# One decoder step: two triples of the gated convolution ahead of q, k, v, and five live delta units

## The chip, the cores and the metric

The kernel runs on one core of one Trainium2 chip. The metric is the device time of one execution in microseconds; lower is better. The core has five engines that take their instructions each from a queue of its own: TensorE (matmuls, PE in the profile, its weight loads PEld), VectorE (DVE), ScalarE (ACT), GpSimd (POOL) and SyncE (SP, which only starts transfers). TensorE writes to PSUM, eight banks that DVE and ACT read; all else lies in SBUF.

## The reference

One layer is computed for 256 prompt tokens and 8 decoding sequences of 4 tokens (288 columns), all in fp32, model width 2048:

```
x += 0.5 * post(SwiGLU_1(pre(x)))
h  = pre(x); P = h @ w_in        # columns [B | C | hc | q | k | v | z | a | b]
y_A = B * dwconv3(C * hc)        # gated convolution, 1024 channels
y_B = gated delta rule over silu(dwconv4(q, k, v)), 8 heads of 128, then rmsnorm * silu(z)
x += post(concat(y_A, y_B) @ w_out)
x += 0.5 * post(SwiGLU_2(pre(x)))
x += post(sigmoid(pre(x) @ w_ple_gate) * (p @ w_ple_proj))
```

B, C, hc, q, k, v and z are each eight blocks of 128 columns. The delta rule goes over chunks of tokens and needs, for each chunk and head, the inverse of a triangular matrix:

```
S_t = e^{g_t} S_{t-1} (I - b_t k_t k_t^T) + b_t k_t v_t^T,   o_t = S_t^T q_t
```

The new states of both convolutions and of the delta rule are outputs too.

## The kernel before

Activations lie transposed: 128 channels on the partitions, 288 tokens along the row. Every weight matrix is cut into 128 x 128 tiles, and the host lays them out in the order in which they are used, four tiles to a chunk of 256 KB. `Feed` loads chunks on SP's queue, six buffers deep, and splits each: ACT copies it in a rounded form (hi, line 133), DVE subtracts (lo, line 134); four split buffers. A tile costs three matmuls of 288 columns, hi with the high and the low part of the activations (lines 361 and 362) and lo with the high part (line 364), so a chunk costs twelve. `gemm_steps` (line 328) goes through the chunks; a block of columns m has a PSUM accumulator while its 16 row tiles k run, and then `done(m, ...)` reads it. Before the matmuls of a chunk it may advance a generator `extra` by some steps (line 352). `gemm_order` (line 66) puts the first `group` blocks of a matrix k by k, so that work may start while the normalised input is still being made, and the others block by block, four chunks each.

Mixing runs four gemms. `qkv` has 24 blocks in the order k, q, v of head 0, of head 1 and so on, the first six k by k; `qkv_done` (line 597) multiplies by the norm's row, pads (`padded`, line 553), applies four taps (`conv`, line 566: the first on ACT, three on DVE, line 572) and SiLU. A side product `ab` runs with the first block. `conv` has 24 blocks in triples (C, hc, B of one t), block by block; `conv_done` (line 1024) makes C times the squared row (`gc`, line 1028), hc times that with padding, two taps on DVE, times the row (`cr`, lines 1036 and 1037, on POOL), and at last B times `cr` into Y (line 1039). `z` has 8 blocks. Then `out` multiplies by w_out.

Beside them goes the delta rule as the generator `delta` (line 907). It waits until `ab` is done, waits 16 steps, computes the gates, makes the products k k^T and k q^T of the heads that are done (`products`, line 709), and after the last q, k, v block: scales, then `solve` (line 725), which inverts the 32-wide diagonal parts of 16 matrices at once, row after row, all on DVE (lines 736 to 757, the last makes GXT), and next to it `decode`, the two units of the decoding tokens with their states S loaded on POOL's queue (line 849). Only when the solve is through do the 16 prompt units start. A unit (line 826) is a chain of 9 or 10 steps: transposes (line 834), T from GXT on DVE (line 768) with its transpose p0 (line 774), five small products (`invert`, line 764), the new values (line 877), outputs and states (lines 882, 893). Live generators take turns, one step each, and at most LIVE = 4 live at once. During `qkv` a chunk advances the work by one step; during `conv` and `z` every second chunk (EVERY) advances it by RATE x EVERY = 4 steps. What is left after z runs on its own.

PSUM: five banks tagged `acc` for accumulators, three tagged `sm`; every fourth bank of a unit comes from `acc` (`unit_bank`, line 205). The program is written in this order, but a planner sets the final order on each engine by its own costs and by when operands are ready: an engine may take an instruction ahead of earlier ones that are not ready in the planner's reckoning. On the chip each engine then keeps to its queue.

Of the kernel before, what the change touches and what calls it, by code (L numbers as in the profile page):

```python
# [7 lines left out]
F32 = mybir.dt.float32  # L8
F32R = mybir.dt.float32r
AF = mybir.ActivationFunctionType  # L10
ALU = mybir.AluOpType
# [17 lines left out]
RAW_BUFS = 6  # L29
SPLIT_BUFS = 4  # L30
GROUP = 5
WIDE = 7
RATE = 2
LIVE = 4
EVERY = 2
PROJ = ((0, 3), (3, 6), (6, 8))
FILL = 3
QUIET = 32
# [34 lines left out]
def orders():  # L73

    gu = []
    for q in range(NQ):
        gu += gemm_order(range(q * 2 * QF, (q + 1) * 2 * QF), KD, WIDE if q == 0 else 0)
    qkv = [m for h in range(H) for m in (32 + h, 24 + h, 40 + h)]  # L80
    conv = [m for t in range(8) for m in (8 + t, 16 + t, t)]
    return {
        "gu": gu,
        "dn": [(m, q * QF + k) for q in range(NQ) for m in range(KD) for k in range(QF)],
        "qkv": gemm_order(qkv, KD, GROUP + 1),
        "conv": gemm_order(conv, KD, 0),
        "z": gemm_order(range(48, 56), KD, 0),
        "out": gemm_order(range(KD), KD, GROUP),
        "proj": gemm_order(range(KD), 2, 0),
        "gate": gemm_order(range(KD), KD, WIDE),  # L90
    }
# [54 lines left out]
def tile_hymba_step(ctx: ExitStack, tc: tile.TileContext, a: dict):  # L146
# [18 lines left out]
    SA = pers.tile([P, 8, NB, 2], F32, name="SA")  # L165

    plan = []
    for name in ("ffn1", "proj0", "qkv", "conv", "z", "out", "proj1", "ffn2", "proj2", "gate"):
        if name[:4] == "proj":
            plan.append((a["proj"], range(*PROJ[int(name[4])])))  # L170
            continue
        if name[:3] != "ffn":
            plan.append((a[name], range(a[name].shape[0])))
            continue
        for q in range(NQ):
            for w in (a["gu" + name[3]], a["dn" + name[3]]):
                n = w.shape[0] // NQ
                plan.append((w, range(q * n, (q + 1) * n)))
# [26 lines left out]
    def unit_bank(name):  # L205

        turn[0] += 1
        if turn[0] % 4:
            return small(name)
        return psum.tile([P, 512], F32, tag="acc", bufs=ACCS, name=name)  # L210

# [116 lines left out]
    def gemm_steps(order, kt, rhs, done, prep=None, extra=None, rate=0, side=None, every=1, fill=(), fine=False):  # L328

        acc, seen, ready = {}, {}, 0
        for c in range(len(order) // CH):
            if prep:
                if c == 0:
                    prep(0)
                    ready = 1
                    feed.split(0)
                if ready == KD:  # L340
                    prep.after()
                upto = max(k for _, k in order[: (c + LEAD) * CH])
                while ready <= upto:
                    prep(ready)
                    ready += 1
                if c == 0:
                    feed.behind = prep.first
                    for _ in fill:
                        pass
                    feed.behind = None  # L350
            hi, lo = feed.next()
            for _ in range(rate * every if c and c % every == 0 else 0):
                next(extra, None)
            for i in range(CH):
                m, k = order[c * CH + i]
                if m not in acc:
                    acc[m] = small(f"acc{m}") if len(acc) >= ACCS else psum.tile([P, 512], F32, tag="acc", bufs=ACCS, name=f"acc{m}")
                    seen[m] = 0
                xh, xl = rhs(k)
                o = acc[m][:, :N]  # L360
                nc.tensor.matmul(o, hi[:, i, :], xh, start=seen[m] == 0, stop=False)  # L361
                nc.tensor.matmul(o, hi[:, i, :], xl, start=False, stop=False)  # L362
                seen[m] += 1
                nc.tensor.matmul(o, lo[:, i, :], xh, start=False, stop=seen[m] == kt)  # L364
# [256 lines left out]

    def dtile(tag, shape=(P,), bufs=LIVE):
        return dl.tile([P, *shape], F32, tag=tag, bufs=bufs, name=tag)
# [137 lines left out]
    S1, started = {}, set()  # L761
    updates = []

    def invert(u, T, TT):

        col = slice(u, u + 1)
        L = LQ[:, u, 0, :]
# [6 lines left out]
        nc.tensor.transpose(p0[:, 0:P], T, ID)  # L774
        nc.scalar.copy(TT, p0[:, 0:P])
        yield
        B = dtile("B")
        nc.gpsimd.memset(B, 0.0)
        ev = lambda x: x.rearrange("p (a i b) -> p a i b", a=2, i=2)[:, :, 0, :]
        od = lambda x: x.rearrange("p (a i b) -> p a i b", a=2, i=2)[:, :, 1, :]  # L780
# [45 lines left out]
    def unit(u):  # L826
# [3 lines left out]
        vT = VD[:, 4 * w : 4 * w + 4, :].rearrange("p h t -> p (h t)") if dec else V[:, h, n * P : (n + 1) * P]  # L830
        col = slice(u, u + 1)
        T, TT = dtile("T"), dtile("TT")
        pt = unit_bank("pt")
        nc.tensor.transpose(pt[:, 0:P], vT, ID)
        nc.tensor.transpose(pt[:, P : 2 * P], kq[:, 0, :], ID)
# [2 lines left out]
        nc.scalar.activation(rv, pt[:, 0:P], AF.Copy, scale=BRK[:, col])  # L838
        nc.scalar.activation(kd, pt[:, P : 2 * P], AF.Copy, scale=KDC[:, col])
        yield  # L840
        yield from (invert4 if dec else invert)(u, T, TT)

        qs = None
        if dec:
# [25 lines left out]
                nc.tensor.matmul(pS[c], kq[:, c, :], S1[h], start=True, stop=True)  # L870
        if dec or n == 1:
            nc.vector.scalar_tensor_tensor(rv, pS[0], CKS[:, col], rv, op0=ALU.mult, op1=ALU.add)
            qs = dtile("qs", bufs=2)
            nc.scalar.activation(qs, pS[1], AF.Copy, scale=EGC[:, col])
            yield
        pn = unit_bank("pn")
        nc.tensor.matmul(pn[:, 0:P], TT, rv, start=True, stop=True)  # L877
        vn = dtile("vnD", bufs=2) if dec else dtile("vn")
        nc.scalar.copy(vn, pn[:, 0:P])
        yield  # L880
        po = unit_bank("po")
# [131 lines left out]
        yield from proj  # L1013
        keep(0, PJ0)

    gemm(ORD["qkv"], KD, x_parts, qkv_done, mix, work, 1, ab_side, fill=fill_mix())
    mrow = mix.value


    r2 = tmp.tile([P, N], F32, tag="diag", bufs=1, name="r2")  # L1020
    nc.vector.tensor_tensor(r2, mrow, mrow, op=ALU.mult)
    part = {}

    def conv_done(m, ps):
        t = m % 8
        if m // 8 == 1:
            part["g"] = tmp.tile([P, N], F32, tag="e1", name="gc")
            nc.vector.tensor_tensor(part["g"], ps, r2, op=ALU.mult)
        elif m // 8 == 2:
            e, dec = padded(ps, part.pop("g"), SA[:, t, :, :], 2)  # L1030
            nc.gpsimd.tensor_copy(CAP[:, t, :], e[:, SEQ : SEQ + 2])
            nc.gpsimd.tensor_copy(SA[:, t, :, :], dec[:, :, 4:6])
            cp, cd = conv(e, CAW[:, t, :], 2)
            part["c"] = b = tmp.tile([P, N], F32, tag="e0", name="cr")
            seq = lambda x: x[:, SEQ:N].rearrange("p (b t) -> p b t", b=NB)
            nc.gpsimd.tensor_tensor(b[:, 0:SEQ], cp, mrow[:, 0:SEQ], op=ALU.mult)
            nc.gpsimd.tensor_tensor(seq(b), cd, seq(mrow), op=ALU.mult)
        else:
            nc.vector.tensor_tensor(Y[:, t, :], ps, part.pop("c"), op=ALU.mult)

    gate_load = marks[-1]
    gemm(ORD["conv"], KD, x_parts, conv_done, None, work, RATE, every=EVERY)
    nc.gpsimd.dma_start(a["conv_qkv_p"], CQP)
    nc.gpsimd.dma_start(a["conv_qkv_s"], SQ)
    nc.gpsimd.dma_start(a["conv_a_p"], CAP)
# [10 lines left out]
        nc.scalar.activation(VD[:, h, :], t[:, SEQ:N], AF.Silu)  # L1056
        finished.append(m)

    gemm(ORD["z"], KD, x_parts, z_done, None, work, RATE, every=EVERY)
    for _ in work:  # L1060
        pass
    YH = big.tile([P, 2, 8, N], F32R, tag="H", name="YH")
# [189 lines left out]
```

## Time and profile before

| | |
|---|---|
| median of 3 runs | 2382.6 us (2380.88 to 2384.11) |
| profiled execution | 2383.07 us, its span 2381.3 us |
| granted TensorE clock, mean | 0.997 |
| instructions in the span | 47494 |
| HBM read, written | 386.68 MB, 9.26 MB |

The span runs from the first to the last instruction. The page gives for every engine its busy time and its share of the span. A stretch from 40 equal slices shows where an engine is full. Groups of instructions carry the line of the kernel, output and inputs by name, the count, busy us, the mean ns of one, and the idle time ahead of them with what ended it. A wait is put down to what came last before the waiting instruction. Mixing lies between about 855 and 1305 us of the span.

### The profile page before, as it was taken

To read this page: it belongs to the slowest core of one execution; us is meant where nothing else is said; L and a number is where in the kernel's file an instruction comes from. 1 tells how busy PE (TensorE), PEld (TensorE's weight loads), DVE (VectorE), ACT (ScalarE), POOL (GpSimd) and SP (SyncE) were. 2 spreads that over 40 slices of the span, in tenths; PEclk is the share of its full clock that TensorE was granted. 3 is DMA by queue.
4 is the path that set the end of the run, shared out by engine and by line. 5 is a ranking of instruction groups with operands and counts; after the bars stand their busy time and mean duration, and the time that the engine had idled before them with its cause. 6 is when DMAs were issued, how large, how long until landed. Compare 5 with 4: busy or idle time off the path is not lost.

```text
span 2381.3 us, 47494 instructions
## 1 busy us (share of the span) xinstructions
PE 2357.7 (99%) x17904; PEld 2336.5 (98%) x17904; DVE 1473.1 (62%) x2788; ACT 1165.9 (49%) x2222; POOL 147.4 (6%) x283
## 2 busy tenths in 40 slices
PE   9999999999999999999999999999999999999997
PEld 9999999999999999999999999999999999999997
DVE  6554555555555688888556577655555555555695
ACT  6444443444444567544455455544443444444474
POOL 0000000000000003122110002430000000000001
PEclk9999999999999999999999999999999999999999
DMA  7665665566656555565444566775656666666654
GB/s 233 172 165 166 167 166 167 165 168 165 167 166 167 166 161 147 162 188 162 129 140 129 167 174 175 226 216 165 168 165 166 167 167 165 166 167 166 187 156 124
DMA packets 213238, 399.07 MB, mean 168 GB/s; under 512 B 24183, under 2 KB 25616, under 8 KB 213008
## 3 DMA queue, kind: packets, MB, share of 16 engines
q1 hardware_dynamic: 207792, 377.73, 56.3%
q0 software_dynamic: 5072, 18.24, 2.5%
q8 instruction: 140, 2.29, 0.4%
q14 instruction: 90, 0.74, 0.1%
q10 hardware_dynamic: 144, 0.07, 0.0%
HBM read 386.68 MB, written 9.26 MB: 166 GB/s over the span
## 4 chain that ended last, share of the span: by engine, by line
PE 60%; DVE 1%; issue 0%; DMA 0%; ACT 0%; POOL 0%; DVEq 0%; ACTq 0%
PE acc L361 19%; PE acc L364 19%; PE acc L362 19%; DVE lo L134 0%; PE pkq L714 0%; DVE Y L1145 0%; PE po L882 0%; PE p L797 0%; DMA S<-in_state_delta 0%; PE pu L993 0%; PE pn L877 0%; DVE cvout L572 0%; PE p L787 0%; PE pd L893 0%; PE pS L870 0%
## 5 line engine op out<-in xcount | busy, mean ns | idle before, releaser
L134 DVE TENSOR_TENSOR lo<-raw,hi 128x512 fp32r<-128x512 f32 (+1 forms) x1417 | 990.5, 700 | 759.6 <-ACT hi L133 736.8
L133 ACT CAST hi<-raw 128x512 fp32r<-128x512 f32 (+1 forms) x1417 | 876.7, 620 | 1124.2 <-PE acc L362 1009.3
L361 PE MATMUL acc<-XH,hi 128*128 128x288 f32 x4096 | 1217.1, 298 | 2.2 <-ACT hi L133 1.2
L364 PE MATMUL acc<-XH,lo 128*128 128x288 f32 x4096 | 1213.1, 297 | 2.2 <-DVE lo L134 2.0
L362 PE MATMUL acc<-XL,hi 128*128 128x288 f32 x4096 | 1197.0, 292 | 0.0
L362 PEld LDWEIGHTS acc<-XL,hi 128*128 128x128 f32 x4096 | 780.4, 191 | 0.3 <-issue 0.2
L361 PEld LDWEIGHTS acc<-XH,hi 128*128 128x128 f32 x4096 | 770.4, 188 | 9.5 <-ACT hi L133 3.9
L364 PEld LDWEIGHTS acc<-XH,lo 128*128 128x128 f32 x4096 | 768.3, 188 | 3.7 <-DVE lo L134 3.3
L362 PE MATMUL acc<-hl_f,hi 128*128 128x288 f32 x1408 | 415.5, 295 | 0.0
L364 PE MATMUL acc<-hh_f,lo 128*128 128x288 f32 x1408 | 415.3, 295 | 0.0
L361 PE MATMUL acc<-hh_f,hi 128*128 128x288 f32 x1408 | 414.5, 294 | 0.0
L364 PEld LDWEIGHTS acc<-hh_f,lo 128*128 128x128 f32 x1408 | 264.8, 188 | 0.0
L362 PEld LDWEIGHTS acc<-hl_f,hi 128*128 128x128 f32 x1408 | 264.3, 188 | 0.0
L361 PEld LDWEIGHTS acc<-hh_f,hi 128*128 128x128 f32 x1408 | 264.0, 187 | 0.0
L445 DVE TENSOR_TENSOR gu_t<-acc,rows_ffn_f 128x288 f32<-128x288 f32 x176 | 79.9, 457 | 51.9 <-PE acc L364 51.6
L465 DVE TENSOR_TENSOR Y<-Y,acc 128x288 f32<-128x288 f32 x96 | 43.5, 453 | 28.1 <-PE acc L364 28.1
L558 POOL MEMSET cvin<- 128x3 f32 (+1 forms) x32 | 3.3, 102 | 900.9 <-PE acc L364 854.4
L1109 POOL DMA_DIRECT2D PJ<-pj_dram x3 | 1.6, 531 | 665.9 <-PE acc L364 665.9
L451 DVE TENSOR_TENSOR gu_t<-gu_t 128x288 f32<-128x288 f32 x88 | 41.3, 471 | 1.8 <-ACT gu_t L447 1.8
L319 ACT ACTIVATE XH<-X,G 128x288 fp32r<-128x288 f32 x64 | 34.3, 536 | 13.2 <-DVE X L398 12.9
L317 DVE TENSOR_TENSOR hl_f<-gu_t,hh_f 128x288 fp32r<-128x288 f32 x88 | 39.6, 452 | 0.0
L572 DVE SCALAR_TENSOR_TENSOR cvout<-cvin,CW,cvout 128x312 f32<-128x312 f32 x72 | 37.4, 536 | 2.9 <-ACT cvout L570 2.3
(369 smaller groups left out, 1239.3 us busy)
## 6 DMA issues: line engine op xcount, KB each, us to landing
raw<-in_gu SPq DMA_DIRECT2D x703, 256.0 KB, 2.7
raw<-in_dn SPq DMA_DIRECT2D x352, 256.0 KB, 2.7
raw<-in_qkv SPq DMA_DIRECT2D x96, 256.0 KB, 2.7
raw<-in_conv SPq DMA_DIRECT2D x96, 256.0 KB, 2.7
raw<-in_out SPq DMA_DIRECT2D x64, 256.0 KB, 2.7
raw<-in_gate SPq DMA_DIRECT2D x64, 256.0 KB, 2.7
raw<-in_z SPq DMA_DIRECT2D x32, 256.0 KB, 2.6
S<-in_state_delta POOLq DMA_DIRECT2D x8, 512.0 KB, 5.5
```

The costliest lines, as they stand in the source:

```text
L133: self.hi = nc.scalar.copy(hi[:, r], t[:, r]).ins
L134: nc.vector.tensor_tensor(lo[:, r], t[:, r], hi[:, r].bitcast(F32), op=ALU.subtract)
L317: nc.vector.tensor_tensor(lo, src, hi.bitcast(F32), op=ALU.subtract)
L319: first = nc.scalar.activation(hi, src, AF.Copy, scale=gain).ins
L361: nc.tensor.matmul(o, hi[:, i, :], xh, start=seen[m] == 0, stop=False)
L362: nc.tensor.matmul(o, hi[:, i, :], xl, start=False, stop=False)
L364: nc.tensor.matmul(o, lo[:, i, :], xh, start=False, stop=seen[m] == kt)
L445: nc.vector.tensor_tensor(t, ps, prep.value, op=ALU.mult)
L451: nc.vector.tensor_tensor(t, t, s, op=ALU.mult)
L465: nc.vector.tensor_tensor(Y[:, m, :], Y[:, m, :], ps, op=ALU.add)
L558: nc.gpsimd.memset(e[:, 0:w], 0.0)
L572: nc.vector.scalar_tensor_tensor(c[:, 0:n], e[:, j : j + n], wcols[:, j : j + 1], c[:, 0:n], op0=ALU.mult, op1=ALU.add)
```

## The change

The first 24 chunks of `conv` (AHEAD: two triples, six blocks, k by k) run ahead of `qkv`; they take over the preparation of the input, the side product and the waiting fill. All 24 blocks of `qkv` then run block by block, and the other six triples of `conv` behind them, then z as before. The squared row is made when the first conv block is done. `cr` moves from POOL to DVE. LIVE is 5, and the delta work gets 5 steps every second chunk of `conv` and `z`. To make room in SBUF, the scratch matrix B of `invert` lies in the buffer that later takes the new values (vn), and qs lies in T. Two of five unit banks come from `acc` instead of one of four. The host packs the w_in tiles in the new order.

```diff
+AHEAD = (GROUP + 1) * KD // CH
-RATE = 2
-LIVE = 4
+LIVE = 5
 EVERY = 2
+STEPS = 5
...
-        "qkv": gemm_order(qkv, KD, GROUP + 1),
-        "conv": gemm_order(conv, KD, 0),
+        "qkv": gemm_order(qkv, KD, 0),
+        "conv": gemm_order(conv, KD, GROUP + 1),
...
-    for name in ("ffn1", "proj0", "qkv", "conv", "z", "out", "proj1", "ffn2", "proj2", "gate"):
+    for name in ("ffn1", "proj0", "conv0", "qkv", "conv1", "z", "out", "proj1", "ffn2", "proj2", "gate"):
+        if name[:4] == "conv":
+            n = a["conv"].shape[0]
+            plan.append((a["conv"], range(AHEAD) if name == "conv0" else range(AHEAD, n)))
+            continue
...
-        if turn[0] % 4:
+        if turn[0] % 5 not in (0, 2):
             return small(name)
...
-            for _ in range(rate * every if c and c % every == 0 else 0):
+            for _ in range(rate if c and c % every == 0 else 0):
                 next(extra, None)
...
-    def invert(u, T, TT):
+    def invert(u, T, TT, B):
...
-        B = dtile("B")
         nc.gpsimd.memset(B, 0.0)
...
         T, TT = dtile("T"), dtile("TT")
+        vn = dtile("vnD", bufs=2) if dec else dtile("vn")
...
-        yield from (invert4 if dec else invert)(u, T, TT)
+        yield from invert4(u, T, TT) if dec else invert(u, T, TT, vn)
...
-            qs = dtile("qs", bufs=2)
+            qs = T
...
-        vn = dtile("vnD", bufs=2) if dec else dtile("vn")
...
-    gemm(ORD["qkv"], KD, x_parts, qkv_done, mix, work, 1, ab_side, fill=fill_mix())
-    mrow = mix.value
-    r2 = tmp.tile([P, N], F32, tag="diag", bufs=1, name="r2")
-    nc.vector.tensor_tensor(r2, mrow, mrow, op=ALU.mult)
-    part = {}
+    part, squared = {}, []
     def conv_done(m, ps):
-        t = m % 8
+        t, mrow = m % 8, mix.value
+        if not squared:
+            squared.append(tmp.tile([P, N], F32, tag="diag", bufs=1, name="r2"))
+            nc.vector.tensor_tensor(squared[0], mrow, mrow, op=ALU.mult)
...
-            nc.gpsimd.tensor_tensor(b[:, 0:SEQ], cp, mrow[:, 0:SEQ], op=ALU.mult)
-            nc.gpsimd.tensor_tensor(seq(b), cd, seq(mrow), op=ALU.mult)
+            nc.vector.tensor_tensor(b[:, 0:SEQ], cp, mrow[:, 0:SEQ], op=ALU.mult)
+            nc.vector.tensor_tensor(seq(b), cd, seq(mrow), op=ALU.mult)
...
+    gemm(ORD["conv"][: AHEAD * CH], KD, x_parts, conv_done, mix, work, 1, ab_side, fill=fill_mix())
+    mrow = mix.value
+    gemm(ORD["qkv"], KD, x_parts, qkv_done, None, work, 1)
     gate_load = marks[-1]
-    gemm(ORD["conv"], KD, x_parts, conv_done, None, work, RATE, every=EVERY)
+    gemm(ORD["conv"][AHEAD * CH :], KD, x_parts, conv_done, None, work, STEPS, every=EVERY)
...
-    gemm(ORD["z"], KD, x_parts, z_done, None, work, RATE, every=EVERY)
+    gemm(ORD["z"], KD, x_parts, z_done, None, work, STEPS, every=EVERY)
```

More of the change, by code (lines that the diff above doesn't have):

```diff
@@ L1014, in fill_mix @@
         keep(0, PJ0)
-    gemm(ORD["qkv"], KD, x_parts, qkv_done, mix, work, 1, ab_side, fill=fill_mix())
-    mrow = mix.value
-    r2 = tmp.tile([P, N], F32, tag="diag", bufs=1, name="r2")
-    nc.vector.tensor_tensor(r2, mrow, mrow, op=ALU.mult)
-    part = {}
+    part, squared = {}, []
     def conv_done(m, ps):
-        t = m % 8
+        t, mrow = m % 8, mix.value
+        if not squared:
+            squared.append(tmp.tile([P, N], F32, tag="diag", bufs=1, name="r2"))
+            nc.vector.tensor_tensor(squared[0], mrow, mrow, op=ALU.mult)
         if m // 8 == 1:
             part["g"] = tmp.tile([P, N], F32, tag="e1", name="gc")
-            nc.vector.tensor_tensor(part["g"], ps, r2, op=ALU.mult)
+            nc.vector.tensor_tensor(part["g"], ps, squared[0], op=ALU.mult)
         elif m // 8 == 2:
```

## The prediction

> **What bounds the kernel now.** I read the page first, then the busy times by stage, then the waits, then the chain of waits around the one place that stands out.
>
> ```profile
> span 2381.3 us, 47494 instructions
> PE 2357.7 (99%) x17904; PEld 2336.5 (98%) x17904; DVE 1473.1 (62%) x2788; ACT 1165.9 (49%) x2222; POOL 147.4 (6%) x283
> PE 60%; DVE 1%; issue 0%; DMA 0%; ACT 0%; POOL 0%; DVEq 0%; ACTq 0%
> ```
>
> TensorE is busy 99% of the span and is the chain. The change adds and removes no gemm matmul, so it can win only what TensorE loses while it waits, runs at a lower clock, or changes between the gemm and the small matmuls of the delta units. All idle time of TensorE together is 2381.3 - 2357.7 = 23.6 us, 1% of the span, and only the mixing stage is touched.
>
> Busy time by stage (columns: stretch, its length, then each engine's busy us with its instructions, TensorE clock, DMA share, GB/s):
>
> ```profile
> 900.00:960.00 60.00, 58.05 (x425) 57.30 (x424) 47.93 (x128) 42.45 (x86) 18.14 (x55) 0.97 0.54 157
> 1020.00:1080.00 60.00, 57.20 (x554) 53.92 (x556) 54.62 (x146) 26.69 (x59) 18.08 (x44) 1.00 0.65 195
> 1680.00:1740.00 60.00, 60.00 (x456) 60.00 (x455) 34.18 (x58) 27.29 (x48) 0.00 (x0) 1.00 0.59 167
> ```
>
> The last row is an undisturbed gemm: 456 matmuls in 60 us, 0.132 us each, so a chunk of 12 takes 1.58 us. The other two are where mixing loses: one has a clock under 1.00, the other a VectorE (DVE) that is 91% busy. Closer, around 911 us:
>
> ```profile
> 910.00:915.00 5.00, 3.25 (x20) 3.02 (x19) 5.00 (x12) 2.18 (x7) 2.73 (x6) 0.84 0.32 97
> 915.00:920.00 5.00, 5.00 (x33) 5.00 (x32) 3.76 (x9) 2.22 (x6) 1.82 (x5) 0.82 0.67 222
> 920.00:925.00 5.00, 5.00 (x40) 5.00 (x39) 4.65 (x17) 3.10 (x8) 1.16 (x3) 1.00 0.63 164
> ...
> 912.00:913.00 1.00, 0.00 (x0) 0.00 (x0) 1.00 (x3) 0.99 (x4) 0.89 (x2) 1.00 0.00 0
> ...
> 914.00:915.00 1.00, 1.00 (x6) 1.00 (x6) 1.00 (x3) 0.13 (x1) 1.00 (x2) 0.50 0.76 223
> ...
> 917.00:918.00 1.00, 1.00 (x9) 1.00 (x9) 0.39 (x2) 0.30 (x1) 0.25 (x2) 1.00 0.89 274
> ```
>
> And the chain and the waits there:
>
> ```profile
> 909.61 1.98 DVE cvout L572 x5
> ...
> 912.34 0.70 DVE lo L134
> ```
>
> ```profile
> PE acc L364 <- DVE lo L134: 2.0, 2, 1.7
> ...
> PE pkq L714 <- DVE LQ L723: 0.8, 1, 0.8
> ```
>
> TensorE stops for 1.7 us because the low half of a weight chunk (lo) comes late: it stands on DVE behind the convolution taps (cvout) of the first six column blocks of q, k, v, which all finish within two chunks, as they run k by k. Then its clock is 0.50 and returns by 917. The price of both: 53 matmuls in ten microseconds where 80 fit, 27 missing at 8 per us, 3.4 us.
>
> By the Trainium skill, "TensorE: Matmul & The Clock Gate", Part 1 (What's actually happening), the clock falls to half only after an idle window of about 3.4 us; by that rule a pause of 1.7 us costs itself alone and 1.7 us would come back instead of 3.4, and the time by it would be 2380.9. The trace disagrees here, with 0.50 behind a pause of 1.7 us, and the trace decides.
>
> The other waits of mixing fall while DVE solves the triangular systems and the two decode units run:
>
> ```profile
> PE pn L877 <- DVE rv L872: 1.0, 1, 1.0
> PE p L813 <- DVE RKQ L232: 1.0, 1, 1.0
> PE p L822 <- DVE T L819: 0.7, 1, 0.7
> PE pSk L861 <- DMA S<-in_state_delta: 0.5, 1, 0.5
> ```
>
> Together 3.2 us, with 0.8 us for the bank of a product (pkq) above: 4.0 us.
>
> **The change part by part.** *First group.* Its durations on DVE (columns: instructions, busy us, mean ns, idle before):
>
> ```profile
> L134 DVE TENSOR_TENSOR lo<-raw,hi 128x512 fp32r<-128x512 f32 x205 | 143.4, 701 | 75.0 <-ACT hi L133 70.3 <-PE pt L835 2.5 <-PE p L797 0.9
> L572 DVE SCALAR_TENSOR_TENSOR cvout<-cvin,CW,cvout 128x312 f32<-128x312 f32 x72 | 37.4, 536 | 2.9 <-ACT cvout L570 2.3
> ...
> L560 DVE TENSOR_TENSOR cvin<-acc,rows_mix 128x256 f32<-128x256 f32 x24 | 10.0, 418 | 4.3 <-PE acc L364 3.4 <-PE pgt L689 0.6 <-issue 0.3
> ...
> L572 DVE SCALAR_TENSOR_TENSOR cvout<-cvin,CAW,cvout 128x304 f32<-128x304 f32 x16 | 8.4, 527 | 0.5 <-ACT cvout L570 0.3
> ...
> L563 DVE TENSOR_TENSOR cvin<-acc,rows_mix 128x32 f32<-128x32 f32 x24 | 4.3, 178 | 0.0
> ...
> L1028 DVE TENSOR_TENSOR gc<-acc,r 128x288 f32<-128x288 f32 x8 | 3.6, 452 | 1.8 <-PE acc L364 1.8
> ```
>
> Six blocks of q, k, v cost DVE 6 x (418 + 178 + 3 x 536) ns = 13.2 us. Two triples of the gated convolution cost 2 x (gc 452 + cvin 596 + two taps 1054 + cr about 600 + Y about 452) = 6.3 us, with 0.5 us for the squared row, 6.8. Here cr, moved from GpSimd (POOL) to DVE, is an estimate from the same two shapes, 418 and 178. Over 15 us (9.5 chunks) from the group's end DVE then has 6.8, two single q, k, v blocks that follow (4.4) and 9.5 lo of 0.70 (6.7): 17.9 us of work, 2.9 over. Splits run three chunks ahead, 4.7 us, so no wait should form, with 1.8 us to spare. The same sum for before is 24.3, 9.3 over, and the wait is there. Bounds: -3.4 if the wait goes, 0 if the conv group makes one like it. In the new group Y follows its cr at once, so DVE waits for ScalarE (ACT), which makes the first tap, with the next lo behind it; the 1.8 us must hold that too. I take -3.4, as the DVE work there is half.
>
> *cr on DVE later.* Six further triples add 0.6 us each; POOL loses a pair that slows DVE:
>
> ```profile
> 1220.76 0.75 POOL L1036 TENSOR_TENSOR cr<-cvout,rows_mix 128x256 f32<-128x256 f32 x1
> 1221.46 0.72 POOL L1037 TENSOR_TENSOR cr<-cvout,rows_mix 128x32 f32<-128x32 f32 x1
> ```
>
> ```profile
> 1220.90 1.17 DVE L134 TENSOR_TENSOR lo<-raw,hi 128x512 fp32r<-128x512 f32 x1 [0.26 <-ACT hi L133]
> ...
> 1222.87 0.67 DVE L134 TENSOR_TENSOR lo<-raw,hi 128x512 fp32r<-128x512 f32 x1
> ```
>
> A lo beside the pair took 1.17 us against 0.67, so of the 0.6 some 0.5 comes back where the two met, and 0 where they didn't. Cover is there while the prefill units run, where DVE and ACT are both 55% busy:
>
> ```profile
> 1140.00:1280.00 140.00, 140.00 (x1075) 135.69 (x1074) 77.00 (x178) 77.04 (x222) 16.00 (x40) 1.00 0.47 133
> ```
>
> Without that cover, during the solve, three triples add 0.3 to 1.8 us to it (below).
>
> *The later start of the units.* q, k, v end 24 chunks later, so 104 chunks of gemm are left to cover the delta work, not 128. Steps: before, 47 + 15 turns of four, 248; after, 35 + 15 turns of five, 250. The work needs 5 (last products, scales) + 62 (solve: 4 + 1 + 1 + 7 + 24 x 2 + 1) + 22 (decode: 2 x 11) + 152 (16 units, 9 or 10 steps each) + 9 + 8, the same in both, so the tail behind z stays as it is: 0. But units start only after the solve, and the solve is a chain on DVE:
>
> ```profile
> 1090.00:1105.00 15.00, 15.00 (x115) 14.78 (x114) 14.86 (x26) 6.27 (x14) 3.23 (x4) 1.00 0.47 126
> ```
>
> ```profile
> L757 DVE STREAM_TRANSPOSE GXT<-Y x1: 702/702/702, 1105.1 to 1105.1; 128x512 f32<-128x512 f32 x1
> ```
>
> ```profile
> L834 PE MATMUL pt<-C,v x16: 272/272/329, 1122.2 to 1247.4; 128*128 128x128 f32 x16
> ```
>
> ```profile
> 1030.40:1105.80 75.40, 43.08 (x142) 26.75 (x143) 1.00 0.60 180
> 1105.80:1122.10 16.30, 12.12 (x41) 7.67 (x41) 1.00 0.64 185
> ```
>
> The last two rows count one matmul of three per tile (those on L361), four per chunk: from the last q, k, v block to the end of the solve TensorE runs 142 / 4 = 35.5 chunks, and 10.2 more until the first unit's transpose. By steps that is 5 + 62 + 22 = 89, 89 / 4, the 23rd turn, chunk 46, as seen. After, 89 / 5 is the 18th turn, chunk 36; the first matmul that needs the solve (p0) stands one turn later, chunk 38. DVE is 99% busy, so the solve can't come sooner: it ends at chunk 35.5 plus the 0.3 to 1.8 us of cr. Ten chunks of slack become 2.5, 4 us, less cr and less 0.4 for the first unit's T: 1.8 to 3.3 us. Bounds: 0 if it holds; if the solve ends 5 us later than so, up to 3.2 us and a clock price of 1.7 (the 3.4 less the pause of 1.7 above). I take +0.3. The decode steps come closer too (2.5 per turn, not 2): their 3.2 us of waits can vanish or double; I take 0, since they are set by DVE's and the state load's time, not by turns. The wait for pkq keeps its place at chunk 62 of the stage: 0.
>
> *Fewer, larger turns.* 152 unit steps make 31 turns, not 38. What a turn costs beside its matmuls (start, us):
>
> ```profile
> 1282.71 0.29 PE L361 MATMUL acc<-XH,hi 128*128 128x288 f32 x1
> 1282.84 0.38 PE L893 MATMUL pd<-vn,kd 128*128 128x128 f32 x2
> 1282.98 0.38 PE L362 MATMUL acc<-XL,hi 128*128 128x288 f32 x1
> 1283.19 0.29 PE L364 MATMUL acc<-XH,lo 128*128 128x288 f32 x1
> ```
>
> From 1282.71 to 1283.19 stand 0.48 us where two gemm matmuls take 0.26: 0.22 for two small ones. If all of it were the change of kind, 7 turns save 1.5 us; if it is 0.11 per matmul, nothing. I take -0.3, near nothing, as two small matmuls must take some time.
>
> *The rest.* B in vn, qs in T, and vn held from a unit's start: five of each for five units, so no new wait while units live that long; the memset that fills B is the same one. Two of five unit banks now come from the gemm's five: within four chunks that is four and the gemm's own, so a new accumulator may have to wait for the last one's reader; cover is the turn between them, some 1.1 us (five steps of two matmuls at 0.11) against 0.45 us of reading (gc). I take 0; its bound is the second rival below. The loads are the same 192 chunks of w_in on SP's queue in another order; on POOL's queue the conv memsets and state copies of two triples pass ahead of q, k, v, and the S loads stay behind the last q, k, v copy. No engine waits longer for these: 0.
>
> Sum: -3.4 + 0.3 - 0.3 = -3.4 us. The profiled execution took 2383.07 us (span 2381.3 and 1.8 around it), so 2379.7; the median, 2382.6, is 0.5 lower: **2379.2 us**, 0.14% faster. About 0.2% (4.8 us) is what a measurement of this kernel can tell from no change, so the forecast is a small gain inside that bound.
>
> **The rivals.** *More goes than the lo wait.* With q, k, v spread out and POOL out of DVE's way, the 4.0 us of decode and product waits go too: 2379.2 - 4.0 = 2375.2. For it: every one of them ends on DVE or on a load behind POOL's cr. Against: DVE stays saturated in the solve. Chance 0.24.
>
> *The solve comes late: slower.* The step that decides is p0 at chunk 38. If DVE gives the solve less than before and it ends 7 us past that slack, TensorE waits 7 us and then loses 1.7 at half clock: 2379.2 + 8.7 = 2387.9. The wait makes the whole slower from 1.7 us on (1.7 + 1.7 eats the 3.4). For it: 99% busy rows. Against: the solve ran 10 chunks early, which shows that DVE takes it ahead of its place. Banks would cost alike: 26 accumulators at 0.3 us each are 7.8. Chance together 0.17.
>
> *The burst only moves.* Six blocks still finish at once, now with a chain through ACT in it. If a wait like the old one forms, only the turns are left: 2382.6. For it: the row of six remains; against: half the DVE work. Chance 0.15.
>
> **How the numbers follow.** Forecast 0.44, own range 2376.5 to 2381.5 (turns -1.5, solve +2 with no clock loss); the rivals 0.24, 0.17 and 0.15. Faster by over 0.2% means under 2377.8: most of the first rival (0.22) and a quarter of the forecast (0.12), 0.34. Slower means over 2387.4: the later half of the solve rival and of the banks, with a part of worse placing, 0.13. The rest, 0.53, is within. The range of 8 in 10 goes down to 2374.0, just past the first rival, and up to 2386.5, which leaves out the worst of the solve.
>
> **What would show it.** Right: no wait of TensorE for lo between the conv group's end and 20 us later, its clock 1.00 in the stretch, and DVE with half as many taps there; the first p0 within three chunks of the solve's end and with no wait before it; waits of 3 to 4 us left between the last q, k, v block and the first unit. Wrong: a clock under 1.00 anywhere in mixing; a wait of p0 for T; a wait of acc (L361) for the reader of the accumulator before it; or decode waits that are gone.

## The result and the profile after

The changed kernel takes 2395.8 us (median of 4 runs, 2395.1 to 2396.5) against 2382.65 for the kernel before on the same chip: a ratio of 1.0054, 95% interval 1.0041 to 1.0067. It is 13.1 us slower; 2379.2 was forecast, and 2386.5 was the upper end of the range.

The page of the changed kernel begins so:

```profile
span 2394.7 us, 47491 instructions
...
PE 2363.1 (99%) x17904; PEld 2339.4 (98%) x17904; DVE 1475.0 (62%) x2804; ACT 1168.0 (49%) x2222; POOL 136.5 (6%) x267
```

The 13.4 us more of span are 8.0 us of further idle time (2394.7 - 2363.1 = 31.6, before 23.6) and 5.4 us more of "busy". A busy share of 99% hides both kinds of loss, so mixing has to be read by what it leaves over beside the gemm. The next rows are stretches of the kernel before with the gemm's matmuls alone (columns: stretch, length, busy us with their number, clock, DMA share, GB/s):

```profile
850.00:1036.30 186.30, 170.97 (x1209) 0.99 0.55 157
1036.30:1122.20 85.90, 73.65 (x522) 1.00 0.60 181
1122.20:1285.60 163.40, 134.29 (x937) 1.00 0.48 134
```

The same of the changed kernel:

```profile
850.00:1071.30 221.30, 207.68 (x1499) 1.00 0.57 161
1071.30:1150.40 79.10, 58.77 (x402) 0.96 0.54 163
1150.40:1297.90 147.50, 111.26 (x770) 1.00 0.44 123
```

The cuts are the last product (pkq), the first transpose of a prompt unit (pt) and the last state product (pd). An undisturbed gemm matmul takes 60 / 456 = 0.1316 us (the row at 1680 in the prediction). A stretch's length less its matmuls at that rate is its **excess**: what small matmuls, waits and the clock take there. Before: 186.3 - 1209 x 0.1316 = 27.2 us up to the products, 17.2 in the solve with the decode units, 40.1 in the prompt units. After: 24.1, 26.2 and 46.2. From there to 1380 us it is 5.6 and 6.4. So the first stretch won 3.1 us, as forecast in kind; the stage of the decode units (from the last pkq to the first pt of a prompt unit) lost 9.0, the prompt units 6.1, the tail 0.8: together 12.8 of the 13.4.

The forecast gain is there. These are 20 us behind the first six blocks, of before and then of after (columns: stretch, length, busy us and number for PE, PEld, DVE, ACT, POOL, then the clock):

```profile
908.00:928.00 20.00, 18.25 (x125) 17.77 (x124) 18.13 (x50) 12.45 (x28) 7.87 (x23) 0.91 0.48 145
```

```profile
908.00:928.00 20.00, 20.00 (x152) 19.81 (x151) 15.06 (x33) 11.92 (x23) 4.43 (x14) 1.00 0.63 174
```

DVE starts 33 instructions there, not 50, no wait for lo is left and the clock is 1.00. The waits of TensorE in mixing say where the time went instead (columns: what waited for what, us in total, times, longest; pSk are the products with the loaded states S, po a unit's outputs):

```profile
PE p L816 <- DVE LQ L814: 4.8, 1, 4.8
PE pSk L866 <- DMA S<-in_state_delta: 2.9, 2, 2.0
PE po L886 <- ACT vn L883: 2.2, 1, 2.2
PE acc L368 <- DVE lo L135: 1.5, 3, 0.8
PE p L790 <- ACT vn L787: 1.2, 1, 1.2
```

The largest is new. TensorE's timeline of the changed kernel around it (start, us, engine, line, what; in brackets the idle time before it):

```profile
1073.79 0.27 PE L838 MATMUL pt<-C,v 128*128 128x128 f32 x1
1073.89 0.27 PE L839 MATMUL pt<-C,kq 128*128 128x128 f32 x1
1079.01 0.48 PE L816 MATMUL p<-C,LQ 128*128 128x128 f32 x1 [4.84 <-DVE LQ L814]
1079.14 0.59 PE L365 MATMUL acc<-XH,hi 128*128 128x288 f32 x1
...
1082.16 0.43 PE L365 MATMUL acc<-XH,hi 128*128 128x288 f32 x1
1082.40 0.32 PE L366 MATMUL acc<-XL,hi 128*128 128x288 f32 x1
```

The first decode unit's transposition p0 (named p here, L816) stands right behind its pt, with no gemm in between, and its operand LQ is late. From 1079.14 to 1082.40 thirteen matmuls take 3.26 us, not 1.71: half clock, 1.55 us more. A second stretch of half clock, from 1096.1 to 1099.5 us, stands behind the 2.0 us wait for S. The two waits cost 6.2 us more than the same ones before (4.8 and 2.9 against 1.0 and 0.5), and two times 3.4 us at half clock cost 3.4: together a little over the 9.0 that the stage lost. What LQ is behind shows on DVE's timeline of the changed kernel:

```profile
1073.99 0.46 DVE L1030 TENSOR_TENSOR gc<-acc,r 128x288 f32<-128x288 f32 x1
...
1076.09 0.68 DVE L135 TENSOR_TENSOR lo<-raw,hi 128x512 fp32r<-128x512 f32 x1
...
1078.04 0.59 DVE L740 COPY Y<-LQ 32x512 f32<-32x512 f32 x1
1078.66 0.29 DVE L814 TENSOR_TENSOR LQ<-LQ,junk 128x128 f32<-128x128 f32 x1
```

DVE works without a pause through scales, the copies that open the solve (L740) and a lo, and comes to LQ at 1078.66, 4.8 us behind pt. In the kernel before, this wait was 1.0 us (p for RKQ).

### The profile page after: what moved, and what is told of

Read it like the earlier page. It is cut to its first block, busy times and chain, and to the rows that moved or that the text cites. A ratio compares the mean times of both kernels' runs of the same rounds, so it can differ in the third digit from the quotient of the medians.

```text
span 2394.7 us, 47491 instructions
## 1 busy us (share of the span) xinstructions
PE 2363.1 (99%) x17904; PEld 2339.4 (98%) x17904; DVE 1475.0 (62%) x2804; ACT 1168.0 (49%) x2222; POOL 136.5 (6%) x267
```

## The experiments

All medians, with the ratio to the kernel before from the runs on the same chip; the excess columns are worked out as above, from one profile each. A stretch of half clock lasts 3.4 us and so adds 1.7 us of excess, and the same pause has one behind it in some profiles and none in others. Up to the products there is one in before, e2, f2, i2 and j2; in the decode stage in after (two), e1, e2 (two of 6.8 us, in part within the pauses), e3 and h5; in the units in e1, e3 and g1.

| kernel | us | ratio, 95% interval | to products | decode, solve | units | tail to 1380 |
|---|---|---|---|---|---|---|
| before | 2382.65 | | 27.2 | 17.2 | 40.1 | 5.6 |
| after | 2395.78 | 1.0041 to 1.0067 | 24.1 | 26.2 | 46.2 | 6.4 |
| e1 decode later | 2393.96 | 1.0038 to 1.0063 | 23.9 | 23.4 | 45.9 | 6.0 |
| e2 five units, old order | 2398.82 | 1.0058 to 1.0084 | 26.4 | 31.9 | 42.6 | 5.7 |
| e3 four units, new order | 2389.84 | 1.0019 to 1.0042 | 24.1 | 22.2 | 43.6 | 6.1 |
| e4 one bank of four | 2388.97 | 1.0018 to 1.0041 | 24.4 | 19.3 | 45.1 | 6.6 |
| g1 decode in small banks | 2391.72 | 1.0024 to 1.0049 | 24.1 | 19.3 | 48.1 | 6.5 |
| i2 one tile | 2391.53 | 1.0027 to 1.0052 | 25.8 | 19.8 | 46.2 | 6.6 |
| f1 before, two banks of five | 2381.28 | 0.9987 to 1.0004 | 24.7 | 16.7 | 39.8 | 5.6 |
| f2 five units, old order, one of four | 2391.02 | 1.0021 to 1.0046 | 27.5 | 19.1 | 45.3 | 5.9 |
| h3 before, cr on DVE | 2385.64 | 1.0006 to 1.0024 | 25.5 | 19.4 | 40.0 | 5.5 |
| h5 four units, five steps | 2387.96 | 1.0014 to 1.0032 | 24.0 | 21.1 | 44.3 | 5.7 |
| f3 four units, closer turns | 2384.98 | 1.0000 to 1.0018 | 24.1 | 20.6 | 40.2 | 5.8 |
| b4 and state products apart | 2379.86 | 0.9981 to 0.9999 | 24.5 | 16.2 | 40.2 | 5.9 |
| b5 and copies on ACT | 2379.90 | 0.9978 to 0.9996 | 24.3 | 16.2 | 40.1 | 5.8 |
| j1 b4 with cr on POOL | 2380.44 | 0.9983 to 1.0000 | 24.2 | 16.9 | 40.2 | 5.8 |
| j2 before, products apart | 2381.32 | 0.9986 to 1.0004 | 27.3 | 15.9 | 40.1 | 5.6 |

**First theory: the place of the decode units and the waves of five.** Four runs together. e1 lets decode begin three steps later:

```diff
-        live = [solve(solved), decode()]
+        def later():
+            for _ in range(3):
+                yield
+            yield from decode()
+        live = [solve(solved), later()]
```

> Changed kernel, with the two decode units made to begin three steps later, so that the first decode matmuls stand one turn later in TensorE's queue and nothing else moves. Theory 1 (the loss of 13.1 us is made of two parts: 7.9 us between the last q, k, v block and the first prompt unit, because TensorE stands for VectorE's decode values with the clock falling behind it, and 7.5 us in the waves of five units): the wait of 4.8 us of p for LQ goes and the clock price with it, 2395.8 - 4.8 - 1.7 = 2389.3 us, range 2388 to 2391; the unit part stays. Rival (VectorE is simply over its work in this stage, so the wait comes back at the next matmul that needs it): 2395 to 2397, with another wait of 4 to 5 us in the stage.

e2 puts the delta part of the change alone (five units, five steps, banks, shared buffers) into the old order; e3 keeps the new order with four units and four steps; e4 takes back only the rule for banks:

```diff
-        if turn[0] % 5 not in (0, 2):
+        if turn[0] % 4:
```

> Kernel before with its own order of weights (q, k, v first, all of the gated convolution behind) and its multiplications by the row on GpSimd, but with five live units, five steps every second chunk, two of five banks from the gemm's, and the shared buffers: the delta part of the change alone. Theory 1 (loss comes from where steps stand, by turns of five and waves of five): the unit tail of 5 to 8 us appears here too, and some of the decode wait, while the wait for the low half at 911 us (3.4 us) stays: 2387 to 2395 us. Rival (the new order of the gemm, which starts the units 24 chunks later, is what costs): 2381 to 2384, since 24 chunks more are left to cover the steps.

> Changed kernel with four live units and four steps every second chunk, one of four banks from the gemm's: the new order alone. Theory 1: the decode wait of 4.8 us and its clock are gone, as its matmuls stand a turn later again; but 250 steps at four per turn need 125 chunks and 104 are left, so some 40 steps run behind the gemm of z with nothing beside them, at 0.3 to 0.6 us each. 2395.8 - 6.5 - 7.5 + (12 to 24) = 2394 to 2406 us. Rival (the order itself costs by DVE's work, not the steps): the decode wait stays near 5 us.

> Changed kernel with one of four unit banks from the gemm's accumulators, as before, in place of two of five; five live units stay. Theory 1: banks play no part, 2395.8 +- 1 us, the waits of p for LQ and of po for vn unchanged. Rival (banks: an accumulator of the gemm waits for the reader of the one before it, 26 times 0.3 us): 2388 to 2391.

The theory fell in half. One turn later won 1.8 us, not 6.5. The waits of e1:

```profile
PE p L816 <- DVE LQ L814: 3.2, 1, 3.2
```

The bank rule alone, which was to play no part, was worth 6.8 us, and 6.9 in the decode stage by the table, where e4 has neither stretch of half clock. The rival's number was met, but not its mechanism: no accumulator waited for a reader in any list of waits of mixing. The waits with one bank of four:

```profile
PE acc L368 <- DVE lo L135: 1.9, 3, 1.1
PE pSk L866 <- DMA S<-in_state_delta: 1.5, 2, 1.0
PE p L816 <- DVE LQ L814: 1.5, 1, 1.5
```

e2 settles the side on which the loss lies: with the old order, and cr still on POOL, the delta part costs 16.2 us, more than either theory gave. The new order doesn't make the loss; that it gives back the 3.0 us between e2 and after is only so if the parts add, which the table doesn't show (e2 loses more in the decode stage, after in the units). The waits of e2:

```profile
PE pn L877 <- DVE rv L872: 7.0, 1, 7.0
PE p L812 <- DVE LQ L810: 4.8, 1, 4.8
```

e3 came out under its band: its wait of p0 is 1.0 us, but the loads of the state cost 4.4, and the steps that found no place before z's blocks (which need the units started) ran as two groups of 52 and 42 small matmuls without gemm, 43.6 us of units with 1.7 of half clock among them, where 40 and the 12 to 24 us expected for them would make 52 or more.

**Second theory: the fence.** TensorE's list as the planner wrote it, of after and of e4 from the same pt on; the traces have the same order:

```
after: pt, pt, p0, then the next block of the gemm
e4:    pt, pt, then 27 matmuls of the next block, then p0
```

In both lists, and in that of the kernel before, the first writes of all tiles of one ring of banks stand in the order in which the program takes them (105 tiles of the ring acc in after, 83 in before, none out of order). The traces don't name banks, so this is read from the lists alone. A decode product that takes a bank of the gemm's ring is therefore a fence: the next gemm block can't be placed ahead of it. In after, p0 is the second unit tile, gets such a bank, and five steps a turn put it in the same turn as pt, just ahead of a block. In e1 it moved by one block, 48 gemm matmuls, and stood at the head of that one. g1 keeps the first 22 unit banks out of the ring (14 are the decode units', the other 8 belong to the first prompt units, which its expectation overlooked), i2 only that of p0:

```diff
-        if turn[0] % 5 not in (0, 2):
+        if turn[0] % 5 not in (0, 2) or turn[0] == 2:
```

> Changed kernel, but the first 22 unit banks, which are those of the two decode units, never come from the gemm's accumulators; the prompt units keep two of five. What the runs so far showed: with one bank of four from the gemm's in place of two of five the time fell by 6.8 us, nearly all of it in the decode stage, and there the first decode product stood 27 gemm matmuls later in TensorE's queue. New theory, the fence: banks of one ring are first written in the order in which the program takes them, so a decode product in a gemm bank must stand ahead of the next gemm block, and when its operand is late on VectorE the whole gemm stands. By it the wait of 4.8 us of p for LQ goes as in that run, and with it its clock: 2389 us, range 2387.5 to 2390.5, first prompt p0 some 6 to 7 us earlier. Rival (accumulators are scarce, the gemm waits for their readers in the prompt units, where most of the 26 extra ones are): no gain in the decode stage, 2394 to 2397.

> Changed kernel with one bank changed: the second unit tile, p0 of the first decode unit, comes from the small banks instead of the gemm's; every other tile as in the change. Fence theory: with it p0 stands 27 gemm matmuls later in TensorE's queue, the wait of 4.8 us of p for LQ falls to about 1.5, and with its clock 4 to 6.5 us go: 2389 to 2392 us, the first decode unit's later tiles as they were. Rival (many accumulators taken, not this one's place): 2395 to 2396.5.

One bank of one tile is worth 4.3 us by the medians. In the profiles the decode stage falls by 6.4: 3.3 us of wait, and both stretches of half clock, of which the one behind the loads of S need not come from the fence. TensorE's timeline of i2 at the same place:

```profile
1075.64 0.27 PE L839 MATMUL pt<-C,kq 128*128 128x128 f32 x1
1075.67 0.38 PE L365 MATMUL acc<-XH,hi 128*128 128x288 f32 x1
...
1079.19 0.29 PE L368 MATMUL acc<-XH,lo 128*128 128x288 f32 x1
1080.97 0.30 PE L816 MATMUL p<-C,LQ 128*128 128x128 f32 x1 [1.49 <-DVE LQ L814]
1081.03 0.38 PE L365 MATMUL acc<-XH,hi 128*128 128x288 f32 x1
```

LQ is as late as ever (5.3 us behind pt), but 27 gemm matmuls stand in the gap, 1.5 us are left, and the matmuls behind come at 0.13 us: the clock holds. g1 has the decode stage of e4 (19.3), and units that cost 48.1, 1.9 more than in after; 1.7 of that is a half clock from 1234.8 to 1238.2 us, behind the same wait of 2.2 us of po that after has without one.

The fence needs both the bank and the turn. f1 gives the kernel before the bank rule alone, f2 takes it from e2:

> Kernel before with only the bank rule of the change: two of five unit banks from the gemm's, four live units as before. Fence theory: a decode product stands in front of a gemm block and waits for VectorE in the saturated stage: 4 to 8 us slower, 2386 to 2391, with one wait of over 3 us of a decode product (p for LQ or pn for rv) and a clock under 1.00 there. Rival (it takes five live units to run short of banks): 2382 to 2383.5.

> Kernel before in its own order of weights, with five live units, five steps every second chunk and the shared buffers, but one bank of four: what the five units cost without the bank rule. Fence theory: the run with both showed 2398.8, of which waits of 7.0 (pn for rv) and 4.8 (p for LQ) and their clock go: 2386 to 2389; what is left over the time before is the five units (last unit alone, turns that hold two steps of one unit), 3 to 6 us. Rival (five units cost nothing by themselves): 2381 to 2384.

f1 was expected slower and is not: with four steps a turn pt and p0 fall into two turns, p0 takes its bank when the block around it already has its own, and stands 28 gemm matmuls behind pt, as before. f2 against e2 shows the fence in the old order: 12.8 us less in the decode stage. There pn stands 24 gemm matmuls later than in e2 and waits 0.2 us, not 7.0; pn has a small bank, but po, which needs it, has one of the gemm's. That po draws pn ahead of the block was not tried by itself. What is left in f2, 8.4 us over before, is 1.9 there and 5.2 in the units.

**What the units cost.** Each kernel runs 320 small matmuls between the units' first transpose and the last state product, for 40 us of excess wherever four units take turns of four and have room for them (before, f1, f3, b4; e3 above had not) and 42.6 to 48.1 with five. In after, 3.4 of its 6.1 us are two waits, the first where a unit's pn and po fall into one turn, the second in the last unit, which runs alone. TensorE's timeline of after (gemm left out):

```profile
1240.91 0.49 PE L886 MATMUL po<-vn,LQ 128*128 128x128 f32 x2 [2.19 <-ACT vn L883]
...
1287.05 0.33 PE L786 MATMUL p<-T,LQ 128*128 128x64 f32 x2
1288.62 0.43 PE L790 MATMUL p<-TT,vn 128*128 128x64 f32 x2 [1.25 <-ACT vn L787]
```

h5 (four units, STEPS = 5) and f3 (four units, four steps, in three of five chunks and in z two of three) part the lone last unit from turns that don't match the units:

```diff
-            for _ in range(rate if c and c % every == 0 else 0):
+            for _ in range(rate if c and (c % every == 0 if every == 1 else c * 3 % 5 < 3 if every == 2 else c * 2 % 3 < 2) else 0):
```

> New order, one bank of four from the gemm's, four live units, five steps every second chunk. It parts the two readings of the unit stage, which costs 45 to 48 us with five units and 40 with four in the runs so far (320 small matmuls each). If the last unit alone is what costs, four waves of four have none and the stage costs 40 to 41 us: 2384 to 2386 us in all. If turns that do not match the number of live units cost (one unit takes two steps in a turn, the kinds of small matmuls mix), it stays at 43 to 45: 2387 to 2390.

> New order of the gemms, four live units, four steps a turn, one bank of four from the gemm's, and turns spread closer: three of five chunks in the gated convolution, two of three in z, so that the units come in four full waves of four and are through before z ends. Theory (loss is fence plus the fifth wave of one unit, and the new order itself gains the 2 to 3 us that were forecast): like before up to the first prompt unit and 39 us of unit matmuls and changes instead of 44: 2379 to 2383 us. Rival (48 fewer matmuls of cover cost in any arrangement, since the same small matmuls run against fewer gemm matmuls): 2386 to 2389, as with one bank of four alone.

These are the stretches of units in h5 and then in f3, gemm alone:

```profile
1145.00:1290.50 145.50, 114.12 (x769) 1.00 0.44 126
```

```profile
1149.80:1288.30 138.50, 109.27 (x747) 1.00 0.45 128
```

44.3 and 40.2: no lone unit in either, so the turns cost 4 us by themselves. In h5 the 320 small matmuls stand in 51 groups, 17 of them of one or two, in f3 in 43 with three so short; matmuls of two different lines stand side by side 93 and 83 times (after: 110), such of unlike shape 30 and 20 times (after: 45). Which of these the time goes by was only read off, not tried; neither count does it alone, as e2 has 41 groups and 45 such neighbours for 42.6 us, and e4 59 groups and 40 for 45.1. Five units with a turn that always takes one step of each were not tried. f3 met its 40 us and missed its time by the decode stage:

```profile
PE pSk L866 <- DMA S<-in_state_delta: 4.0, 3, 2.2
```

**The state loads.** h3 moves only cr to DVE, in the kernel before; b4 adds to f3 a second yield after each pair of state products (and a later start of the solve's double yields, so that the units keep their place); b5 also moves two copies of the convolution's state from POOL to ACT:

```diff
                                 start=b0 + j == 0, stop=b0 + j == NB - 1, tile_position=(0, 32 * hh),
                             )
                 yield
+                yield
...
-            for _ in range(SOLVE_STEPS if i >= 8 else 1):
+            for _ in range(SOLVE_STEPS if i >= 16 else 1):
```

> Kernel before with one edit of the change: cr, the two multiplications by the row, on VectorE instead of GpSimd. In the runs so far TensorE waited 1.5 to 4.4 us for a state load S wherever cr was on VectorE in the new order, against 0.5 us before. Theory (with cr gone from GpSimd's list the planner counts on the state loads earlier and puts the third pair of state products 24 gemm matmuls behind the first instead of 46, while a load takes about 5 us as ever): a wait of 3 to 4.5 us of pSk for S, 2385 to 2388 us. Rival (the order of the gemms delays the loads, cr plays no part): the wait stays at 0.5 us, 2382 to 2383.5.

> The run with four units in closer turns (2385.0 us), with the decode units yielding twice after each pair of state products, so that these stand 24 gemm matmuls apart, and the solve yielding once per row up to row 15 instead of up to row 7, so that the units start where they did. Theory: the 4.0 us of waits for S go, 2380 to 2382 us. Rival (the loads are late for another reason, such as GpSimd's list, where a load stands behind copies that wait for the convolution): the waits stay at 3 to 4 us, 2384 to 2386.

> The kernel of the run beside it (four units, closer turns, state products apart), and the two small copies of the convolution's state (CAP and SA), for which GpSimd waits 10 to 14 us with a state load behind them, on ScalarE. If GpSimd's list is what makes the loads late: waits for S under 0.5 us and 2379.5 to 2381.5 us. If the loads are only placed too near: as the run beside it, within 1 us.

The waits of h3 for the state:

```profile
PE pSk L861 <- DMA S<-in_state_delta: 1.7, 2, 0.9
PE pSk L861 <- POOL EX L853: 1.4, 1, 1.4
```

Together 3.1 us where it was 0.5. The median is 3.0 us over before, with an interval from 1.4 to 5.7; but the profiled execution is the fastest of h3's eleven (2383.6 of up to 2388.0) and only 0.5 us over that of before: 2.2 more in the decode stage, 1.7 less up to the products, where no half clock came. So about 2 us stand in the profile, and the rest of the median in none. Nearly half of the waits are for EX (the keys and queries in the form that the product takes), which POOL fills, and that was not expected. Cr leaves POOL's list; by the theory the planner then counts on the loads sooner and the trace shows the third pair of products 24 gemm matmuls (3.2 us) behind the first two, not 46 (6.1 us). The loads are no slower in the new order. These are the issues of before and then of e3 (in KB each, then the median us from issue to landing):

```profile
S<-in_state_delta POOLq DMA_DIRECT2D x8, 512.0 KB, 5.5
```

```profile
S<-in_state_delta POOLq DMA_DIRECT2D x8, 512.0 KB, 5.1
```

With the pairs spread in b4 no wait for S is left, the decode stage costs 16.2 us instead of 20.6, and the kernel is under both: 2379.9 us, 15.9 under after and 2.8 under before, where the interval ends just below 1 (0.9999). The waits of b4 in mixing:

```profile
PE acc L368 <- DVE lo L135: 1.4, 2, 1.2
PE p L816 <- DVE RKQ L237: 1.0, 1, 1.0
```

b5 is the same: with the pairs apart, the copies on POOL's list don't matter.

**Is the gain the new order's?** j2 gives the old order the spacing of b4, j1 gives b4 the old place of cr:

> Kernel before in its own order with the two edits of the best run so far (2379.9 us): the decode units yield twice after each pair of state products, the solve yields once per row up to row 15; the units start where they did before. If the gain of that run comes from the new order of the gemms (no wait for lo at 911 us and no half clock behind it), this one stays near before, 2381.5 to 2383 us, with that wait in it. If it comes from the spacing of the state products alone: 2379 to 2380.5.

> The best run so far (new order, four units, closer turns, state products apart) with cr back on GpSimd. The case for cr on VectorE was that GpSimd slows VectorE where the two meet; with the state products apart the planner's reckoning of GpSimd's list matters no more. If VectorE's work in the solve decides: 0.5 to 1.5 us faster, 2378.5 to 2379.5. If the two cancel as forecast: 2379.5 to 2380.5.

j2 lies between its two bands, 1.4 us under before with an interval that holds 1, and keeps its 1.7 us wait for lo at 913 us. Spacing is worth 1.3 us in its decode stage, the new order 2.8 in the first stretch of the two profiles (of which 1.7 is a half clock at 961 us in j2), 1.5 by the medians of b4 and j2, which differ in cr and the turns too. cr on DVE is worth 0.6 us, less than these runs can tell from nothing, once its effect on the place of the products is gone.

## Why the prediction was wrong

*First group, -3.4.* Right in mechanism: no wait for lo behind the conv group, 33 DVE instructions for 50, clock 1.00. That 80 matmuls fit ten microseconds is too many, 76 do by the prediction's own rate; 3.4 holds all the same, as 1.75 us of pause and half of the 3.4 us at half clock (913.4 to 916.8). But the size was one execution's. The pause of 1.74 or 1.75 us stands in all six profiles in the old order, the half clock behind it in three. The first stretch costs 24.7 to 27.5 there (mean 26.4) and 23.9 to 25.8 in the eleven profiles of the new order (mean 24.3): 2.1 us, where the profiled pair shows 3.1. A wait for lo is left at 959 us, 0.8 us in after and 2.5 in i2, with a half clock there.

*Solve, +0.3.* Right where nothing else stood in the way: in e4 the solve ends 1.8 chunks ahead of the first prompt p0 (forecast 2.5). In after it ends 9.3 chunks ahead, so the sign "within three chunks" was not met: p0 comes 6.6 us later than in e4, as TensorE had stood, and the solve ends 5.3 us earlier. That p0 stands at chunk 37.8 (forecast 38) and waits for nothing.

*"I take 0, since they are set by DVE's and the state load's time, not by turns."* This is the step that failed, the decode steps coming closer: +9.0 us, not 0. The waits are set by the operand's time less the place of the product, and turns set the place. 2.5 steps a turn put p0 into the turn of its pt, and the bank rule kept the next block behind it; i2 shows 4.3 us for that tile, e4 6.8 for the whole rule. Of the rest, 2.1 over before in e4, h3 shows that cr alone can make as much.

*"Banks" at 0, with the readers as their bound.* This failed with it, as the fence needs both. The bound was for the wrong thing; its count was near, as of 182 unit banks the rule takes 28 more from the gemm's ring, not 26. No accumulator waited for a reader; the ring's order took away the freedom to put gemm work ahead of a late product. Alone the rule costs nothing that f1 shows, which is why its price can't be read from the kernel before.

*"No engine waits longer for these: 0"*, of the queues. Taking cr off POOL's list moved TensorE's products, not the loads: +3.0 us in h3's median, 2.2 in the decode stage of its profile.

*Fewer, larger turns, -0.3.* The groups of small matmuls fell from 42 to 39, not by the 7 of the forecast, and they cost 0.144 us a matmul instead of 0.125: +6.1 us, 3.4 of it waits; the other 2.7 stay open but for h5, which puts 4 us on turns of five with four units. "The tail stays as it is" came to +0.8. The shared buffers at 0 were right: f3 and b4 have them and their units cost 40.2.

The slower rival named the solve and p0 of the prompt units, and the readers of banks; neither was it. Of the signs listed, "a clock under 1.00 anywhere in mixing" was met twice in after, behind the waits for LQ and for S:

```profile
1075.00:1080.00 5.00, 0.99 (x4) 0.99 (x5) 4.78 (x15) 0.63 (x2) 0.00 (x0) 0.90 0.49 152
1080.00:1085.00 5.00, 4.93 (x29) 4.70 (x28) 4.83 (x12) 1.24 (x2) 0.00 (x0) 0.76 0.00 0
...
1095.00:1100.00 5.00, 3.97 (x66) 3.07 (x66) 1.82 (x6) 0.00 (x0) 1.28 (x2) 0.66 0.52 167
```

## What to carry to other kernels

Where a planner writes each engine's list, ask of every small product not only what it waits for but what may be put in front of it: a bank from the bulk work's own ring, taken just ahead of the next block, turns a wait of 1.5 us, the rest of which the bulk covers, into one of 4.8 with the clock behind it. Try turns and live units together: here four steps for four units cost 40 us where there was room, five for four 44, five for five 42.6 to 48.1, and why is open. Spread products that need a load by the load's landing time. Excess over the bulk matmuls, stage by stage, finds in one table what a busy share of 99% hides.

## What the runs showed of the hardware

The same pause does not always cost the same. h3 runs the old first group and pauses 1.74 us up to 913.1, like the kernel before, whose rows the prediction shows. In h3 these are the five microseconds of the pause, and two single ones behind it:

```profile
910.00:915.00 5.00, 3.26 (x24) 3.02 (x24) 5.00 (x12) 2.62 (x7) 2.76 (x6) 1.00 0.31 95
...
914.00:915.00 1.00, 1.00 (x9) 1.00 (x9) 1.00 (x3) 0.55 (x2) 1.00 (x2) 1.00 0.65 215
915.00:916.00 1.00, 1.00 (x10) 1.00 (x9) 1.00 (x3) 0.18 (x1) 0.75 (x1) 1.00 0.71 156
```

The clock stays at 1.00 where it was 0.50 in the profile of before. Of the six profiles in the old order, all with this pause of 1.74 or 1.75 us, three have the half clock behind it (before, e2, f2) and three don't (f1, h3, j2). Longer ones are no surer: po waits 2.2 us in after and in i2 without it and in g1 with it. Each of the five pauses of 3.2 us or more in mixing was followed by half clock (after's 4.84: 13 matmuls at 0.25 us). Nor does it take one long pause: e3 has 3.4 us of half clock at 1261.8 us, behind 5 us of small unit matmuls alone, with no pause over 0.5 us.

The Trainium skill, "TensorE: Matmul & The Clock Gate", Part 1 (What's actually happening), says that the clock falls after at least one idle window of about 3.4 us, and that this window runs freely. The length agrees: a stretch of half clock lasted 3.4 us here, or 6.8. That a whole window must be idle does not, as 1.75 us sufficed three times. That the pause's place in the window decides would fit the three of six, but no run here moved the one against the other. So in these profiles such a pause cost 1.75 us, and 1.7 us more in half of them.
